# Moving the sample's 32 columns to the second token tile, and a third tile whose two parts share one 512-column product

## The chip, the core and the metric

One core of a Trainium2 chip runs the whole program. The metric is device time in microseconds of one execution, the median over runs. The engines are named as in the profile: PE is the matrix engine (TensorE; its weight loads have a row PEld of their own), DVE is VectorE, ACT is ScalarE, SP issues most of the DMAs.

## The reference

One inference step of a two-layer encoder runs for two groups of tokens that share all weights: 1024 rows of a new stream (the prompt) and 32 rows of a running one (the sample), D = 1024 each. Each layer has a mixer and a feed-forward part, with norms and per-group modulation around them:

```python
for i in range(DEPTH):                      # DEPTH = 2
    mod = jax.nn.silu(c) @ w_ada[i] + b_ada[i]
    h = rmsnorm(x, g_norm[i, 0]) * (1 + sc1) + sh1
    # layer 0: u, v = split(gelu(h @ w_in)); mix = (u * (W_s rmsnorm(v) + b)) @ w_out
    # layer 1: trailing means over 2, 4, 8, 16 rows minus h, a linear map per group
    x = x + gt1 * rmsnorm(mix, g_norm[i, 1])
    h = rmsnorm(x, g_norm[i, 2]) * (1 + sc2) + sh2
    f = jnp.square(jax.nn.relu(h @ ffn_w_up[i])) @ ffn_w_down[i]
    x = x + gt2 * rmsnorm(f, g_norm[i, 3])
```

The sample's pooling also reads 15 cached rows. Outputs are both groups' results, the last 15 pooling inputs of each, and the sample's normalised v rows. All arrays are float32.

## The kernel before

**Layout.** Activations lie transposed: channels on partitions (8 blocks of 128), tokens along the free dimension. Three token tiles are kept in SBUF all the time (`TILES`, line 27): prompt columns 0 to 383, 384 to 767, and 768 to 1023 followed by the 32 sample columns, so 384, 384 and 288 columns. `acc0` to `acc2` hold the residual stream or the running sum of a tile, with 16 columns of halo in front for the pooling.

**Precision.** Every weight block and every activation is split in a rounded large part and a small rest (`hh` and `hl`, `wh` and `wl`). `products` (line 897) makes three matmuls for each term: large by large (line 902), large weight by small activation (903) and small weight by large activation (904), all summed in one PSUM bank. A weight block of 128 x 128 is loaded for each matmul.

**Work.** A feed-forward chunk of 512 hidden channels on one tile is an item, `ffn_item` (line 1281): four up products of 8 terms, each read by ACT (relu, then square) and split into `fh` and `fl`, and eight down products of 4 terms, each added to `acc` by `accumulate` (the first chunk of a layer writes by ACT instead). `sgu_item` (line 1156) does the same for the gating mixer, with the gating products of v between. The down products of an item are emitted behind the first up product of the next item (`pending`, `flush`). `passes` (lines 318 to 325) lists the chunks: in each layer some chunks run on all tiles one after the other, and most run on one tile alone, tile by tile (layer 0: chunks 0, 1 and 4 to 7; layer 1: chunks 0 to 3, and 6 and 7 for the third tile). A weight item is loaded by DMA and split by one ACT and one DVE step of 1024 columns a partition; 16 slots hold 8 such pairs.

**Order.** What lies between the parts of a layer (norms, residual, modulation, pooling, output transposes) is written as generators, the fillers. The emission order is decided while the program is built, by a planner that adds up a matrix-engine time and a DVE time:

```python
def tick(us):
    time["pe"] += us
    time["dve"] = max(time["dve"], time["pe"] - 4.0)
tt = on_dve(nc.vector.tensor_tensor, 0.16, 930.0)   # 0.16 + elements / 930
...
while time["dve"] < time["pe"] and fillers:          # in weave(), after each product
    if not pull():
        break
```

`weave` first takes a weight step from the stream and then pulls filler steps, from the first two fillers in the list, as long as the DVE account is behind. `run_ffn` (line 1539) sees to it that a tile's filler is complete before the tile's first chunk of the next part: if it isn't, the pending down products are flushed and the rest of the filler is emitted there (`finish`). For layer 1, a tile's filler is `to_pool`: residual, norm, pooling, the group products (`pp`, line 1529), then `mix_to_ffn` with a second residual and the modulation that writes `hh` and `hl`. Its steps name the tiles `r_rf`, `r_r_1x`, `r_rp` (norm factors), `xo` (old residual), `win` (windows). The last output blocks are transposed by `turn_last` (`LAST`, line 106) and scaled into `xlast`.

Of the kernel before, what the change touches and what calls it, by code (L numbers as in the profile page):

```python
# [26 lines left out]
TILES = [(0, 384, 0), (384, 384, 0), (768, 256, DEC)]  # L27
# [7 lines left out]
def tile_stream_encoder_step(  # L35
# [66 lines left out]
    acc = [const.tile([P, KB, HALO + n], F32, name=f"acc{t}") for t, n in enumerate(ncol)]  # L102
# [3 lines left out]
    LAST = [(0, 0, P), (P, 0, P), (ncol[-1] - P, P - DEC, DEC)]  # L106
# [5 lines left out]
    one = work.tile([P, 384], F32, tag="c", bufs=3, name="one")  # L112
# [13 lines left out]
    def A(t, kb, c0=0, w=None):  # L126
        w = ncol[t] - c0 if w is None else w
        return acc[t][:, kb, HALO + c0 : HALO + c0 + w]


    def room(part, t, name, dtype=F32):
        return work.tile([P, KB, ncol[t]], dtype, tag=f"h{part}{t}", bufs=1, name=name)

# [9 lines left out]
    def t_m(name):  # L143
        return work.tile([P, 384], F32, tag="m", bufs=3, name=name)

    def t_c(name):
        return work.tile([P, 384], F32, tag="c", bufs=3, name=name)
# [188 lines left out]
    for q in range(4):  # L336
        for j in (8 + 2 * q, 9 + 2 * q, 2 * q, 2 * q + 1):
            add_ada(0, j)
        add_w(*v_item(0, q))
        if q == 0:  # L340
            for b in range(3, 6):
                add_x(b)
    first_ada = len(stream)
    for b in range(6, 9):
        add_x(b)
# [30 lines left out]
    def in_raw(k):  # L376
# [4 lines left out]

    x_rows = [
        room("h", t, f"x_rows{t}")
        .rearrange("p k n -> p (k n)")[:, : ncol[t] // P * D]
        .rearrange("p (b k n) -> p b k n", k=KB, n=P)
        for t in range(NT)
    ]
    junk = room("l", NT - 1, "xsq")
# [176 lines left out]
    def x_squares(b, r):  # L565
# [5 lines left out]
            accum_out=ssx[:nr, b : b + 1],  # L571
        )

    def x_turn(b, r):
        t = min(b // 3, 2)
        c0 = (b - 3 * t) * P
        nr = P if b < 8 else DEC
        for half in range(2):
# [6 lines left out]
            dst = acc[t][:, half * 4 : half * 4 + 4, HALO + c0 : HALO + c0 + nr]  # L585
# [150 lines left out]
    class Stat:  # L736
# [7 lines left out]
        def square(self, k, src=None):  # L744

            if k == 0:
                self.sq = room("l", self.t, f"sq_{self.tag}")
# [27 lines left out]
            if k + w == KB and self.split:  # L775
                self.parts = [
                    work.tile([P, 384], F32R, tag=g, bufs=3, name=f"s{g}_{self.tag}") for g in "cm"
# [12 lines left out]
        def finish(self, out):  # L790
# [7 lines left out]
            r = work.tile([P, 384], F32, tag="rr", bufs=2, name=f"r_{self.tag}")[:, :n]  # L798
# [9 lines left out]
    def residual(st, l, cf, tag, out, store=True, stat=True):  # L808
# [12 lines left out]
        for half in range(2):  # L821
            for k2 in (2 * half, 2 * half + 1):
                load(k2)
            for k2 in (2 * half, 2 * half + 1):
# [12 lines left out]
                a = acc[t][:, 2 * k2 : 2 * k2 + 2, HALO:]  # L837
# [4 lines left out]
        if store:  # L842
            nc.sync.dma_start(xd[t], acc[t][:, :, HALO:])
# [9 lines left out]
    def apply(t, l, cf, sh, r, keep=False):  # L853
        hh[t] = room("h", t, f"hh{l}_{cf}_{t}", F32R)
        hl[t] = room("l", t, f"hl{l}_{cf}_{t}", F32R)
        parts = [[(k, *seg) for seg in segs[t]] for k in range(KB)]
        if keep and len(segs[t]) == 1:
            parts = [parts[k] + parts[k + 1] for k in range(0, KB, 2)]
        for part in parts:
            xs = []  # L860
            for k, c0, w, v in part:
                x = A(t, k, c0, w)
                a = t_m(f"mt{t}_{k}_{v}")[:, :w] if keep else x
# [23 lines left out]
    def first_norm(t):  # L887
        n = ncol[t]
        nb = 3
        cp = t_c(f"r_h0_{t}")  # L890
        got = []
        yield from spread(t, ssx[:, 3 * t : 3 * t + nb], f"h0_{t}", got, cp)
# [4 lines left out]
    def products(ps, n, terms):  # L897

        last = len(terms) - 1
        tick(3 * len(terms) * (0.004 + n / 2265.0))  # L900
        for i, (wh, wl, rh, rl) in enumerate(terms):
            mm(ps[:, :n], wh, rh, start=i == 0, stop=False)  # L902
            mm(ps[:, :n], wh, rl, start=False, stop=False)  # L903
            mm(ps[:, :n], wl, rh, start=False, stop=i == last)  # L904
# [86 lines left out]
    with tc.manual_schedule():  # L991
# [14 lines left out]
        for q in range(4):  # L1006
# [4 lines left out]
            if q == 0:  # L1011
                stream_to("x", 5)
# [3 lines left out]
                next(h1)  # L1016
                x_turns.popleft()()
# [12 lines left out]
        stream_to("x", 8)  # L1030
# [19 lines left out]
    for half in range(2):  # L1050
        x = work.tile([P, 384], F32R, tag="rr", bufs=2, name=f"hs{half}")[:, : 8 * DEC].rearrange(
# [3 lines left out]
        nc.vector.tensor_copy(x[:, :, 0:DEC], hh[NT - 1][:, ks, 256 : 256 + DEC])  # L1055
        nc.vector.tensor_copy(x[:, :, DEC:], hl[NT - 1][:, ks, 256 : 256 + DEC])
# [19 lines left out]
    for p, b in v_order:  # L1076
# [3 lines left out]
        if p == 2 and b < NT:  # L1080
            with tc.issue_after(loads[("v", 2, 3)]):
                nc.sync.dma_start(xd[b], acc[b][:, :, HALO:])
# [34 lines left out]
    def t_hid(kind, name):  # L1117
        return work.tile([P, 384], F32R, tag="h" + kind, bufs=5, name=name)

    def split(dst_hi, dst_lo, src, n):  # L1120
        act(out=dst_hi[:, :n], in_=src[:, :n], func=AF.Copy)  # L1121
        tt(out=dst_lo[:, :n], in0=src[:, :n], in1=dst_hi[:, :n].bitcast(F32), op=ALU.subtract)

    def accumulate(t, d, ps, first):
        n = ncol[t]
        if first:
            act(out=A(t, d), in_=ps[:, :n], func=AF.Copy)
        else:
            tt(out=A(t, d), in0=A(t, d), in1=ps[:, :n], op=ALU.add)

    def up_terms(wkey, t):
        wh, wl = need_w(wkey)
        return [
            (wh[:, k * P : (k + 1) * P], wl[:, k * P : (k + 1) * P], hh[t][:, k, :], hl[t][:, k, :])
# [21 lines left out]
    def sgu_item(p, t, mix, after):  # L1156
# [8 lines left out]
        def inputs(g):  # L1165
# [5 lines left out]
            if nsm:  # L1171
                nc.sync.dma_start(
                    vl[:nsm, nch, :], vd[SEQ : SEQ + nsm, g * 256 : (g + 1) * 256]
                )
# [14 lines left out]
        def up(g, k):  # L1189
# [3 lines left out]
            products(ps, n, up_terms(("u", p, g, k), t))  # L1193
# [5 lines left out]
            act(out=u[:, :n], in_=ps[:, :n], func=AF.Gelu_apprx_tanh)  # L1199
            us.append(u)  # L1200

        def gate(g):
# [4 lines left out]
            for k in range(2):  # L1207
# [10 lines left out]
                if nsm:  # L1218
                    mm(
                        sp[:, npr : npr + nsm],  # L1220
                        vl[:nsm, nch, k * P : (k + 1) * P],
# [4 lines left out]
            for k, sp in enumerate(sps):  # L1226
                f = 2 * g + k
                s = t_c(f"s{g}_{t}_{k}")
                stt(
                    out=s[:, :npr].rearrange("p (c j) -> p c j", j=P),  # L1230
# [438 lines left out]
```

## Time and profile before

| what | value |
|---|---|
| median of 3 runs | 2206.56 us (2206.07 to 2206.97) |
| span of the profiled execution, first to last instruction | 2201.9 us |
| own time of the profiled execution | not recorded beside its span; the median is 4.7 us above the span |
| mean granted PE clock over the span | 0.999 |
| ACT busy | 986.7 us (45%) |
| HBM traffic | 278.95 MB read, 31.84 MB written, 141 GB/s |

A timeline row has the start in us, the length in us, the engine, the line, the operation, what is written from what, shapes, and how many instructions were merged in it. A group row ends in busy us, the mean ns of one, and the idle time before it with what ended it. Line 79 is the helper through which DVE operations are recorded.

### The profile page before, as it was taken

What the parts mean: (1) busy time and instruction counts of PE and PEld (TensorE: products, weight loads), DVE (VectorE), ACT (ScalarE), POOL (GpSimd) and SP (SyncE); (2) the same over time, 40 slices, a digit from 0 to 9 for tenths busy, and PEclk for the clock granted to TensorE, in tenths of its full rate; (3) what the DMA queues carried; (4) which work ended last, traced back from release to release, by engine and by line L of the source; (5) the groups of instructions that cost most, each with busy time, mean ns of one, the idle gap of its engine ahead of it and who ended that gap; (6) DMA issues with size and microseconds to landing.
All of it is one profiled execution on the core that took longest, in us unless ns stands there. A gap on an engine that the chain in (4) does not pass through costs nothing.

```text
span 2201.9 us, 33431 instructions
## 1 busy us (share of the span) xinstructions
PE 2178.7 (99%) x13383; PEld 2096.0 (95%) x13383; DVE 1376.8 (63%) x2433; ACT 986.7 (45%) x1679; POOL 0.7 (0%) x6
## 2 busy tenths in 40 slices
PE   7999999999999999999999999999999999999998
PEld 5777899999999999999999999999999999999998
DVE  5665746566869556575747879879675553523375
ACT  4633422134447552323445566656564542313354
POOL 0000000000000000000000000000000000000000
PEclk9999999999999999999999999999999999999999
DMA  8475624243527443343645465555454552302343
GB/s 296 128 250 165 201 81 135 89 143 113 154 82 222 148 145 124 102 131 122 191 125 153 149 182 177 180 185 159 139 171 143 155 153 66 107 10 77 97 121 111
DMA packets 354976, 312.98 MB, mean 142 GB/s; under 512 B 10818, under 2 KB 316682, under 8 KB 354820
## 3 DMA queue, kind: packets, MB, share of 16 engines
q1 hardware_dynamic: 352676, 309.43, 45.3%
q8 instruction: 105, 1.72, 0.3%
q10 hardware_dynamic: 2144, 1.41, 0.2%
q14 instruction: 51, 0.42, 0.1%
HBM read 278.95 MB, written 31.84 MB: 141 GB/s over the span
## 4 chain that ended last, share of the span: by engine, by line
PE 96%; DMA 2%; DVE 1%; ACT 1%; SPq 0%; issue 0%; ACTq 0%; DVEq 0%
PE pf L902 12%; PE pf L904 11%; PE pg L902 11%; PE pg L904 11%; PE pg L903 11%; PE pf L903 11%; PE pu L902 3%; PE pu L904 3%; PE po L902 3%; PE po L904 3%; PE po L903 3%; PE pu L903 3%; PE pv L929 2%; PE pv L930 2%; PE pv L931 2%; PE psp L1211 1%
## 5 line engine op out<-in xcount | busy, mean ns | idle before, releaser
L902 PE MATMUL pf<-hh,wh_up 128*128 128x384 f32 (+1 forms) x1536 | 502.6, 327 | 0.0
L902 PE MATMUL pg<-fh,wh_dn 128*128 128x384 f32 (+1 forms) x1536 | 498.0, 324 | 0.0
L904 PE MATMUL pf<-hh,wl_up 128*128 128x384 f32 (+1 forms) x1536 | 496.5, 323 | 0.0
L904 PE MATMUL pg<-fh,wl_dn 128*128 128x384 f32 (+1 forms) x1536 | 494.8, 322 | 0.0
L903 PE MATMUL pg<-fl,wh_dn 128*128 128x384 f32 (+1 forms) x1536 | 494.6, 322 | 0.0
L903 PE MATMUL pf<-hl,wh_up 128*128 128x384 f32 (+1 forms) x1536 | 490.5, 319 | 0.0
L902 PEld LDWEIGHTS pg<-fh,wh_dn 128*128 128x128 f32 x1536 | 288.8, 188 | 4.4 <-issue 3.3
L79 DVE TENSOR_TENSOR wl_up<-raw,wh_up 128x1024 fp32r<-128x1024 f32 x152 | 185.9, 1223 | 167.8 <-ACT wh_up L417 167.8
L902 PEld LDWEIGHTS pf<-hh,wh_up 128*128 128x128 f32 x1536 | 288.2, 188 | 1.3 <-issue 0.8
L903 PEld LDWEIGHTS pg<-fl,wh_dn 128*128 128x128 f32 x1536 | 288.6, 188 | 0.7
L903 PEld LDWEIGHTS pf<-hl,wh_up 128*128 128x128 f32 x1536 | 288.6, 188 | 0.4
L904 PEld LDWEIGHTS pg<-fh,wl_dn 128*128 128x128 f32 x1536 | 288.5, 188 | 0.0
L904 PEld LDWEIGHTS pf<-hh,wl_up 128*128 128x128 f32 x1536 | 287.9, 187 | 0.0
L417 ACT ACTIVATE wh_up<-raw 128x1024 fp32r<-128x1024 f32 x152 | 161.1, 1060 | 278.6 <-PE pf L903 214.3
L79 DVE TENSOR_TENSOR acc<-acc,pg 128x384 f32<-128x384 f32 (+1 forms) x336 | 173.9, 518 | 165.7 <-PE pg L904 164.4
L417 ACT ACTIVATE wh_dn<-raw 128x1024 fp32r<-128x1024 f32 x152 | 161.0, 1060 | 217.7 <-PE pg L903 180.4
L79 DVE TENSOR_TENSOR wl_dn<-raw,wh_dn 128x1024 fp32r<-128x1024 f32 x152 | 185.9, 1223 | 85.3 <-ACT wh_dn L417 85.1
L79 DVE SCALAR_TENSOR_TENSOR aa<-raw,csil,aa 128x512 f32<-128x512 f32 (+1 forms) x364 | 204.3, 621 | 1.9 <-DMA raw<-in_w_ada_dram 1.5
L1293 ACT ACTIVATE r<-pf 128x384 f32<-128x384 f32 (+1 forms) x192 | 86.8, 452 | 197.1 <-PE pf L904 191.7
L79 DVE TENSOR_TENSOR fl<-r,fh 128x384 fp32r<-128x384 f32 (+1 forms) x192 | 100.3, 522 | 104.6 <-ACT fh L1121 103.4
L902 PE MATMUL pu<-hh,wh_u 128*128 128x384 f32 (+1 forms) x384 | 128.0, 333 | 0.0
L902 PE MATMUL po<-ush,wh_o 128*128 128x384 f32 (+1 forms) x384 | 124.2, 324 | 0.0
(264 smaller groups left out, 2899.6 us busy)
## 6 DMA issues: line engine op xcount, KB each, us to landing
raw<-in_ffn_w_up_dram SPq DMA_DIRECT2D x152, 512.0 KB, 4.1
raw<-in_ffn_w_down_dram SPq DMA_DIRECT2D x152, 512.0 KB, 3.4
raw<-in_w_ada_dram SPq DMA_DIRECT2D x96, 512.0 KB, 3.9
raw<-in_sgu_w_in_dram SPq DMA_DIRECT2D x40, 512.0 KB, 4.6
xd<-acc SPq DMA_DIRECT2D x8, 1536.0 KB, 7.4
raw<-in_sgu_w_out_dram SPq DMA_DIRECT2D x24, 512.0 KB, 4.1
xo_r<-xd SPq DMA_DIRECT2D x32, 384.0 KB, 3.3
vd<-vt SPq DMA_DIRECT2D x32, 256.0 KB, 3.3
```

The lines of the kernel that those rows point to most:

```text
L79: return op(out, *args, **kw)
L417: act(out=wh, in_=r, func=AF.Copy)
L902: mm(ps[:, :n], wh, rh, start=i == 0, stop=False)
L903: mm(ps[:, :n], wh, rl, start=False, stop=False)
L904: mm(ps[:, :n], wl, rh, start=False, stop=i == last)
L929: mm(ps[:m, :], a_h, wh[:, o : o + 512], start=k == 0, stop=False)
L930: mm(ps[:m, :], a_h, wl[:, o : o + 512], start=False, stop=False)
L931: mm(ps[:m, :], a_l, wh[:, o : o + 512], start=False, stop=k == KB - 1)
L1211: mm(sp[:, c * P : (c + 1) * P], vl[:, c, k * P : (k + 1) * P], wr[:, c * P : (c + 1) * P], start=True, stop=True,)
L1293: act(out=r[:, :n], in_=ps[:, :n], func=AF.Relu)
```

## The change

The 32 sample columns go from the third tile to the second, so the tiles have 384, 416 and 256 columns. For the third tile the large and the small part of an activation are kept side by side (`double_room`, and one `hid` tile per hidden block). The large weight part multiplies both at once, a matmul of 512 columns that fills a PSUM bank; the small weight part multiplies the large activation part, 256 columns, into the first half. The two halves are then added where a sum leaves PSUM: `gather` for up products, two adds in `accumulate` for down products.

```diff
-TILES = [(0, 384, 0), (384, 384, 0), (768, 256, DEC)]
+TILES = [(0, 384, 0), (384, 384, DEC), (768, 256, 0)]
+WIDE = 384 + DEC
+X_ORDER = (0, 1, 2, 3, 4, 5, 8, 6, 7)
...
-    LAST = [(0, 0, P), (P, 0, P), (ncol[-1] - P, P - DEC, DEC)]
+    LAST = [(0, 0, P), (P, 0, P)]
...
-    def products(ps, n, terms):
-
+    def products(t, ps, terms):
+
+        n = ncol[t]
         last = len(terms) - 1
-        tick(3 * len(terms) * (0.004 + n / 2265.0))
+        tick(len(terms) * ((3 if t < NT - 1 else 2) * 0.004 + 3 * n / 2265.0))
         for i, (wh, wl, rh, rl) in enumerate(terms):
-            mm(ps[:, :n], wh, rh, start=i == 0, stop=False)
-            mm(ps[:, :n], wh, rl, start=False, stop=False)
-            mm(ps[:, :n], wl, rh, start=False, stop=i == last)
+            if t < NT - 1:
+                mm(ps[:, :n], wh, rh, start=i == 0, stop=False)
+                mm(ps[:, :n], wh, rl, start=False, stop=False)
+                mm(ps[:, :n], wl, rh, start=False, stop=i == last)
+            elif i < last:
+                mm(ps, wh, rl, start=i == 0, stop=False)
+                mm(ps[:, :n], wl, rh, start=False, stop=False)
+            else:
+                mm(ps[:, :n], wl, rh, start=False, stop=False)
+                mm(ps, wh, rl, start=False, stop=True)
+
+    def gather(t, ps, out, func):
+        n = ncol[t]
+        if t == NT - 1:
+            act(out=out, in_=ps[:, n : 2 * n], func=AF.Copy)
+            tt(out=out, in0=out, in1=ps[:, :n], op=ALU.add)
+            act(out=out, in_=out, func=func)
+        else:
+            act(out=out, in_=ps[:, :n], func=func)
...
     def accumulate(t, d, ps, first):
         n = ncol[t]
+        parts = [ps[:, :n], ps[:, n : 2 * n]] if t == NT - 1 else [ps[:, :n]]
         if first:
-            act(out=A(t, d), in_=ps[:, :n], func=AF.Copy)
-        else:
-            tt(out=A(t, d), in0=A(t, d), in1=ps[:, :n], op=ALU.add)
+            act(out=A(t, d), in_=parts.pop(), func=AF.Copy)
+        for x in parts:
+            tt(out=A(t, d), in0=A(t, d), in1=x, op=ALU.add)
```

In `products`, the operand named `rl` of the third tile is both parts side by side. Along with this:

- The sample's rows are loaded and turned with the second tile's (block 8 ahead of blocks 6 and 7), its first norm and its separate steps (its own coefficients, its cached rows and pooling windows, its state outputs) move to the second tile's norm and filler, and the second tile's output gets a fourth block.
- The 16 halo columns leave `acc`. A `halo` tile carries the end of one tile's pooling input to the next, and the first level of each window is made in two or three steps instead of one.
- The gating step writes its sum back to PSUM and the product to the up tile, where a tile of its own was used before; the sample's rows of v come by a DMA into a tile of their own. Tiles of 384 columns become 416 wide, and one tag has 2 buffers instead of 3.
- The queue of passes, the planner's rules and its DVE constants stay.

More of the change, by code (lines that the diff above doesn't have):

```diff
@@ L860, in apply @@
             xs = []
+            kept = {k: t_m(f"mt{t}_{k}") for k, *_ in part} if keep else {}
             for k, c0, w, v in part:
                 x = A(t, k, c0, w)
-                a = t_m(f"mt{t}_{k}_{v}")[:, :w] if keep else x
+                a = kept[k][:, c0 : c0 + w] if keep else x
                 stt(
@@ L1467, in run @@
-            parts = [(acc[t][:, :, 0 : HALO + npr], npr, 0, "p")]
+            yield 0.5 if nsm or t == NT - 1 else False
+            if nsm or t == NT - 1:
+                if nsm:
+                    src, out_ap, nm = pool_ext["e"][:, :, 32:48], state_pool_sample[0, 0], "s"
+                else:
+                    src, out_ap, nm = acc[t][:, :, npr - 16 : npr], state_pool_prompt[0, 0], "p"
+                for half in range(2):
+                    so = t_x(f"stp_{nm}{half}", [P, 512])
+                    pt = ps_ms(f"stT_{nm}{half}")
+                    tick(0.5)
+                    for i in range(4):
+                        nc.tensor.transpose(
+                            pt[:16, i * P : (i + 1) * P], src[:, half * 4 + i, :], ident
+                        )
+                    nc.vector.tensor_copy(so[:16, :], pt[:16, :])
+                    nc.sync.dma_start(out_ap[:, half * 512 : (half + 1) * 512], so[1:16, :])
+                yield False
```

208 lines of the change are left out of this document (115 added, 93 removed).

## The prediction

> **What bounds the kernel now.** I read the page first, then the timeline of the matrix engine to get the distance between starts of products of each width, then the groups of VectorE and ScalarE with shapes kept apart, then busy time by stretch around the place where layer 0 hands over to layer 1.
>
> ```profile
> span 2201.9 us, 33431 instructions
> ...
> PE 2178.7 (99%) x13383; PEld 2096.0 (95%) x13383; DVE 1376.8 (63%) x2433; ACT 986.7 (45%) x1679; POOL 0.7 (0%) x6
> ...
> PE 96%; DMA 2%; DVE 1%; ACT 1%; SPq 0%; issue 0%; ACTq 0%; DVEq 0%
> ```
>
> The matrix engine is never free and carries 96% of the chain, so the change is worth what it takes from the sequence of products, less whatever makes that sequence wait. The recorded length of a product (0.29 us for 288 columns) overlaps the next one; what counts is the distance between starts:
>
> ```profile
> 799.95 0.29 PE L902 MATMUL pf<-hh,wh_up 128*128 128x288 f32 x1
> ...
> 801.95 0.30 PE L902 MATMUL pf<-hh,wh_up 128*128 128x288 f32 x1
> ...
> 660.20 0.34 PE L902 MATMUL pf<-hh,wh_up 128*128 128x384 f32 x1
> ...
> 663.88 0.34 PE L902 MATMUL pf<-hh,wh_up 128*128 128x384 f32 x1
> ...
> 149.63 0.40 PE L929 MATMUL pv<-wh_v,hh 128*128 128x512 f32 x1
> ...
> 152.41 0.40 PE L929 MATMUL pv<-wh_v,hh 128*128 128x512 f32 x1
> ...
> 2177.11 1.07 PE L1615 MATMUL yT<-ident,acc 128*128 128x128 f32 x8
> 2177.94 0.38 PE L902 MATMUL pg<-fh,wh_dn 128*128 128x288 f32 x1
> ```
>
> 15 products of 288 columns take 2.00 us, 133.3 ns each; 21 of 384 take 3.68 us, 175.2 ns; 12 of 512 take 2.78 us, 231.7 ns; 8 transposes of 128 columns take 0.83 us, 104 ns.
>
> **Products of the third tile.** From 288 to 384 columns a product grows by 41.9 ns in 96 columns, 0.4365 ns a column, and 7.6 ns are left at no columns. The line gives 231.1 ns at 512, and 231.7 was measured, so it holds there; it gives 119.3 ns at 256 and 189.2 ns at 416. One term (a weight block with its two parts) takes 3 x 133.3 + 3 x 175.2 = 925.5 ns on the third and second tile now, and 3 x 189.2 + 231.1 + 119.3 = 918.0 ns after: the columns are the same, one start in six goes, and 7.5 ns with it. The third tile has 2 layers x 8 chunks x 64 terms in the feed-forward part and 256 in the gating mixer (16 products of 8, 32 of 4): 1280 terms, 9.6 us. Bounds: if a 256-column product keeps the 133.3 ns of a 288-column one, 14 ns a term are lost against this, and the sum is 8 us the other way; if it falls to the 104 ns of a transpose, the gain is 29 us. I stay on the line, because the 512 point lies on it.
> The Trainium skill, "TensorE: Matmul & The Clock Gate", section "Wait — 56ns, not 53.3ns?", has starts of warm products apart by columns over 2.4 GHz plus about 2.5 ns. The trace disagrees: 120 + 2.5 against 133.3 ns, 213.3 + 2.5 against 231.7. By that rule a removed start is worth 2.5 ns, 3.2 us in all in place of 9.6.
>
> **What the small engines get.** The third tile's sums now lie in two halves of a PSUM bank. An up product was read by one ScalarE step; now a copy, an add on VectorE, and the function. A down product was added once; now twice.
>
> ```profile
> L79 DVE TENSOR_TENSOR wl_dn<-raw,wh_dn 128x1024 fp32r<-128x1024 f32 x152 | 185.9, 1223 | 85.3 <-ACT wh_dn L417 85.1
> ...
> L79 DVE TENSOR_TENSOR acc<-acc,pg 128x384 f32<-128x384 f32 x224 | 123.7, 552 | 138.0 <-PE pg L904 137.0
> ...
> L79 DVE TENSOR_TENSOR acc<-acc,pg 128x288 f32<-128x288 f32 x112 | 50.3, 450 | 27.7 <-PE pg L904 27.4
> ...
> L79 DVE TENSOR_TENSOR fl<-r,fh 128x288 fp32r<-128x288 f32 x64 | 29.3, 457 | 5.7 <-ACT fh L1121 4.7
> ```
>
> From 384 to 288 columns an add loses 102 ns, so 256 columns take about 416 ns. A third-tile item of the feed-forward part (4 up products, 8 down products, 8 weight splits) holds VectorE for 8 x 1.223 + 8 x 0.450 + 4 x 0.457 = 15.2 us of its 192 x 0.1333 = 25.6 us on the matrix engine. After it is 9.8 + 24 x 0.416 = 19.8 us of 64 x 0.3504 = 22.4 us. Spare VectorE time per item falls from 10.4 to 2.6 us.
>
> Within an item this should still just flow:
>
> ```profile
> 1342.43 0.45 DVE L79 TENSOR_TENSOR acc<-acc,pg 128x288 f32<-128x288 f32 x1
> 1342.80 1.23 DVE L79 TENSOR_TENSOR wl_dn<-raw,wh_dn 128x1024 fp32r<-128x1024 f32 x1
> 1343.93 0.62 DVE L79 SCALAR_TENSOR_TENSOR hl<-acc,mod,hh 128x384 fp32r<-128x384 f32 x1
> ```
>
> Back to back, steps start closer than they last (0.37 for 0.45, 1.13 for 1.23). Two down products take 8 x 0.3504 = 2.80 us; their VectorE work is one split and four adds, 1.13 + 4 x 0.336 = 2.5 us.
>
> ```profile
> L417 ACT ACTIVATE wh_dn<-raw 128x1024 fp32r<-128x1024 f32 x152 | 161.0, 1060 | 217.7 <-PE pg L903 180.4
> ...
> L1121 ACT ACTIVATE fh<-r 128x288 fp32r<-128x288 f32 x64 | 28.5, 445 | 1.8
> L1295 ACT ACTIVATE r<-r 128x288 f32<-128x288 f32 x64 | 28.4, 444 | 1.8
> ...
> L1293 ACT ACTIVATE r<-pf 128x288 f32<-128x288 f32 x64 | 25.3, 395 | 8.1 <-PE pf L904 8.1
> ```
>
> An up product, 2.80 us, has on ScalarE a weight rounding, the copy, the function, the square and the rounding: 1.060 + 0.395 + 2 x 0.444 + 0.445 = 2.79 us by the 288-column rows, a little less at 256. Copy and add, about 1 us, must free the bank before the next product but one, 2.80 us on; a filler or split on VectorE in front of the add eats that cover. I put 1.5 us in all on such waits, between 0 and 20 (1 us in each of the third tile's 20 items).
>
> **Where the lost spare time was used.** The norms, residuals and pooling between the layers ("fillers") run on VectorE beneath products. The sample's share, and the whole sample window, now belong to the second tile's filler, which is due earlier than the third's.
>
> ```profile
> core 0: us, PE busy (x) PEld busy (x) DVE busy (x) ACT busy (x) POOL busy (x), PEclk, DMA share, GB/s
> 1299.30:1407.10 107.80, 107.80 (x777) 107.80 (x776) 91.49 (x138) 68.92 (x112) 0.00 (x0) 1.00 0.67 204
> 1407.10:1545.40 138.30, 138.30 (x794) 133.51 (x794) 116.15 (x194) 90.59 (x160) 0.00 (x0) 1.00 0.54 166
> 1545.40:1564.20 18.80, 18.76 (x114) 17.89 (x114) 12.70 (x19) 5.67 (x7) 0.00 (x0) 1.00 0.39 117
> ```
> ```profile
> 1491.28 0.61 DVE L79 SCALAR_TENSOR_TENSOR sm_rp<-sq_rp,eps,sc_rp 128x384 fp32r<-128x384 f32 x1
> ...
> 1496.58 1.14 DVE L79 SCALAR_TENSOR_TENSOR acc<-acc,coef,r_rp 128x384 f32<-128x384 f32 x2
> ...
> 1539.46 0.61 DVE L79 SCALAR_TENSOR_TENSOR hl<-acc,mod,hh 128x384 fp32r<-128x384 f32 x1
> ...
> 1564.18 0.34 PE L902 MATMUL pf<-hh,wh_up 128*128 128x384 f32 x1
> ```
>
> The three stretches run from the second tile's last layer-0 down products to its first layer-1 product at 1564.18: then come the third tile's four solo chunks, the first tile's four, and the down products that are flushed because the second tile's filler isn't finished. Its last input is written at 1540.1, 24 us ahead. VectorE is busy 220 of 265 us. After, it gets 4 x 4.6 = 18 us more in the third tile's items and some 18 us more in the second tile's filler (40 steps on 32 columns, the sample's windows, wider rows), and the stretch is 4 x 3.2 = 13 us shorter: 256 of 252 us. It no longer fits unless work of the third tile's filler, also in there, gives way.
>
> ```profile
> L79 DVE TENSOR_TENSOR acc<-acc,xo_r 128x768 f32<-128x768 f32 x32 | 30.4, 949 | 0.0
> ...
> L79 DVE SCALAR_TENSOR_TENSOR hl<-acc,mod,hh 128x384 fp32r<-128x384 f32 x32 | 18.8, 615 | 0.2 <-ACT hh L875 0.2
> ...
> L79 DVE SCALAR_TENSOR_TENSOR acc<-acc,coef,r_rp 128x384 f32<-128x384 f32 x16 | 9.3, 612 | 0.0
> L79 DVE TENSOR_TENSOR sq_r_1x<-sq_r_1x 128x768 f32<-128x768 f32 x9 | 8.6, 951 | 0.0
> ...
> L79 DVE SCALAR_TENSOR_TENSOR hl<-acc,mod,hh 128x32 fp32r<-128x32 f32 x16 | 3.9, 246 | 0.0
> ```
>
> How late it gets is set by the order in which the program's planner emits steps, so I redo its accounts with its own constants, which decide order and stand for no time of mine. An item's 64 terms count 3 x (0.004 + columns/2265) each, its VectorE steps 0.16 + elements/930: 33.3 - 17.0 = 16.3 us are spare at 384 columns, 25.2 - 15.7 = 9.5 at 288, 36.0 - 17.4 = 18.6 at 416 and 22.2 - 20.5 = 1.7 at 256; the last chunk gives some 3.5 to its squares, and a layer's first chunk gains 4.6, since ScalarE writes its sums. Between the first tile's layer 0 and the second tile's layer 1 that is 4 x 16.3 + 34 + 70 = 169 us now (second tile's items, third's, first's) for the steps of the first and the second tile's filler, 66 + 65 = 131. After it is 74 + 3 + 70 = 147 for 67 + 80 = 147. The 38 us of slack that waits and the third tile's filler used are gone, so the second tile's filler should be about 38 planner-us behind when its first item comes. The flushed down products supply 7; what is left, 31, is the filler's entire last part, the residual and the modulation (15.2 + 2.6 + 13.0), and the program then forces it out with nothing else for the matrix engine. On VectorE it is 8 x (0.612 + 0.246) + 4 x 1.02 + (3 x 1.02 + 1.2) + 16 x (0.615 + 0.246) = 29 us of recorded lengths (1.02 is 0.95 widened to 832 columns; 1.2 is for two steps of one width, by the 0.55 and 0.61 us rows), about 24 us at back-to-back spacing (57 steps, 0.085 us each). The first up product, 24 x 0.189 = 4.5 us, follows block by block beneath its end, and the 6 us that VectorE idles in the flushed stretch take some; from the last square to the first scaled step 5.3 us passed in the trace (1491.28 to 1496.58), part of it other work, and I add 4 for that chain. Stall: 24 - 4.5 - 6 + 4 = 17.5, say 18 us, between 0 and 36 (no packing ahead, pooling late too).
>
> **The rest.**
>
> ```profile
> 2195.16 4.19 DVE L79 SCALAR_TENSOR_TENSOR xlast<-yT,r_last,xlast 128x512 f32<-128x512 f32 x6
> ...
> L79 DVE SCALAR_TENSOR_TENSOR hl<-mt,mod,hh 128x32 fp32r<-128x32 f32 x8 | 2.0, 244 | 0.0
> ```
>
> Behind the last product six scaled adds become four, 4.19 x 2/6 = 1.4 us less; a second accumulate adds 0.3: 1.1 us gained. The third tile's final transposes fall from 24 to 16 twice and the second's output rises by 8: 8 x 104 ns = 0.9 us gained. At the start the sample joins the second tile's first norm: 16 VectorE steps of 0.244 us, 3.9 us, partly beneath weights that are being loaded; I take 1 of 0 to 3.9, as products there wait for inputs only at block edges. Moved DMAs (the sample's rows ahead of blocks 6 and 7, the sample's gating rows in a load of their own) are as many as before and small; nothing for them.
>
> Sum: -9.6 - 0.9 - 1.1 + 1 + 1.5 + 18 = +8.9 us on a span of 2201.9. The median of the runs is 2206.56, 4.7 us above the span; the profile carries no time of its own execution, so I add the change to the median: 2215.5 us.
>
> **Rivals.** *It fits* (faster): VectorE's real steps are shorter than the planner's constants (1.13 for 1.26 us), so the forced part may run early in real gaps, and the third tile's filler gives way. Its place is the second tile's first layer-1 product; it decides if the delay stays below the 24 us of cover. Then the stall is 0 and the time 2206.6 - 11.6 + 2.5 = 2197.5. For it: 45 idle us in the three stretches; against: much of that idleness is waiting in the filler's own chain, which doesn't pack. *Half a stall*: 6 to 14 us, 2204 to 2211, no change to be measured. *The weight load bounds the narrow product*: a 256-column product can't go below the load of the next weights; at 133.3 ns a term loses 14 ns, 18 us, and even without the stall the time is 2215. Against it: transposes, with as large a load each, start 104 ns apart, below 119. The Trainium skill, same page, section "LDWEIGHTS (loading the stationary operand)", has 128 columns load in 128/1.2 = 106.7 ns; by it 119 ns clears the load, and the trace's 104 ns agree. *Banks come free late* in every third-tile item: 20 x 1 us, about 2216 without the big stall, more with it.
>
> **How the numbers follow.** The stall decides: 0.50 for a stall of 14 us or more, 2211 to 2236; 0.25 for it fits; 0.15 for half a stall; 0.05 each for the load and for the banks. The range from 2196 to 2236 runs over all of them; the likeliest case alone spans 2211 to 2236. A measurement here can tell about 0.2%, 4.4 us, from no change. Faster by more than that is it fits, 0.25; within, half a stall, 0.15; slower, the other three, 0.60.
>
> **What would show it.** Starts 512 columns apart by 229 to 232 ns and 256 by 118 to 121 in the third tile's items; a third-tile chunk of 22.4 us; VectorE at nine tenths there; and one gap of 10 to 30 us on the matrix engine ahead of the second tile's first layer-1 up product, ended by VectorE or ScalarE writing its input. Wrong if that gap isn't there, or if the gaps lie between third-tile products and end at the accumulate or the gather.

## The result, and the profile after

The changed kernel takes 2243.05 us (median of 4 runs, 2241.23 to 2244.38) against 2206.4 us of the kernel before on the same chip: a ratio of 1.0165, 95% interval 1.0151 to 1.0179. It is slower, as forecast, but by 36.7 us where 8.9 were forecast, and outside the range of 2196 to 2236 us. The page of the profile after:

```profile
span 2239.4 us, 31192 instructions
...
PE 2184.1 (98%) x12091; PEld 2029.6 (91%) x12091; DVE 1458.6 (65%) x2713; ACT 1011.0 (45%) x1753; POOL 0.7 (0%) x6
...
PEclk9999999999999999999999999999799999999999
...
PE 92%; DVE 3%; DMA 2%; ACT 1%; issue 1%; ACTq 0%; DVEq 0%; SPq 0%
```

There are 1292 products fewer, yet the matrix engine is busy 5 us longer; VectorE has 82 us more work; and one slice in 40 has a granted clock of 7 tenths. Line 81 is here the helper for VectorE steps that was line 79. The matrix engine's waits (engine, tile and line waiting, releaser, us in total, times, longest) begin with a new one:

```profile
PE pn_r_1x L809 <- ACT sc_r_1x L794: 23.3, 1, 23.3
...
PE pf L923 <- ACT hh L894: 3.9, 1, 3.9
...
PE pg L930 <- ACT f L1160: 0.7, 1, 0.7
PE pg L927 <- DVE acc L81: 0.7, 1, 0.7
```

Both large ones lie at one place, ahead of the second tile's first layer-1 up product. The timeline of the matrix engine there:

```profile
1570.89 0.34 PE L925 MATMUL pg<-f,wl_dn 128*128 128x384 f32 x1
1571.06 0.35 PE L809 MATMUL pn_rp<-sc_rp,ones 128*128 128x416 f32 x1
1571.26 0.45 PE L809 MATMUL pn_rp<-sm_rp,ones 128*128 128x416 f32 x1
1594.99 0.72 PE L809 MATMUL pn_r_1x<-sc_r_1x,ones 128*128 128x416 f32 x1 [23.29 <-ACT sc_r_1x L794]
1595.68 0.72 PE L809 MATMUL pn_r_1x<-sm_r_1x,ones 128*128 128x416 f32 x1
1600.35 1.06 PE L923 MATMUL pf<-hh,wh_up 128*128 128x416 f32 x2 [3.95 <-ACT hh L894]
...
1604.21 0.35 PE L924 MATMUL pf<-hl,wh_up 128*128 128x416 f32 x1
```

From 1571.3 to 1600.35 the engine has two small products to do (the two `pn_r_1x`). The norm of the mixer's output (`rp`) has only just been summed, so residual, second norm and modulation all lie in the gap. VectorE does this in it:

```profile
1571.11 0.69 DVE L81 SCALAR_TENSOR_TENSOR acc<-win2p,acc 128x512 f32<-128x512 f32 x1
...
1572.18 0.68 DVE L81 TENSOR_TENSOR win2p<-acc 128x510 f32<-128x510 f32 x1
...
1578.34 0.61 DVE L81 SCALAR_TENSOR_TENSOR acc<-acc,coef,r_rp 128x384 f32<-128x384 f32 x1
...
1583.03 1.02 DVE L81 TENSOR_TENSOR acc<-acc,xo_r 128x832 f32<-128x832 f32 x1 [0.18 <-DMA xo_r<-xd]
...
1592.62 1.65 DVE L81 TENSOR_TENSOR sq_r_1x<-sq_r_1x 128x832 f32<-128x832 f32 x2 [0.96 <-ACT sq_r_1x L763]
1594.98 0.65 DVE L81 SCALAR_TENSOR_TENSOR sm_r_1x<-sq_r_1x,eps,sc_r_1x 128x416 fp32r<-128x416 f32 x1 [0.71 <-ACT sc_r_1x L794]
1597.56 0.59 DVE L81 SCALAR_TENSOR_TENSOR q_r_1x<-pn_r_1x,q_r_1x 128x416 f32<-128x416 f32 x1 [1.94 <-ACT q_r_1x L814]
```

The steps named `win2p` are the third tile's windows: they stand in the queue between the second tile's steps. From 1571.4 to 1600.3 some 17 us are the second tile's own steps, 6 us the third tile's windows, 1.6 us a weight split and an add, and 4 us idle time in the chain, of which the three bracketed waits for ScalarE make 3.6.

### The profile page after: what moved, and what is told of

Same layout as the page of the kernel before. It is cut to its first block, busy times and chain, and to the rows that moved or that the text cites. A ratio compares the mean times of both kernels' runs of the same rounds, so it can differ in the third digit from the quotient of the medians.

```text
span 2239.4 us, 31192 instructions
## 1 busy us (share of the span) xinstructions
PE 2184.1 (98%) x12091; PEld 2029.6 (91%) x12091; DVE 1458.6 (65%) x2713; ACT 1011.0 (45%) x1753; POOL 0.7 (0%) x6
## 4 chain that ended last, share of the span: by engine, by line
PE 92%; DVE 3%; DMA 2%; ACT 1%; issue 1%; ACTq 0%; DVEq 0%; SPq 0%
PE pf L923 8%; PE pg L923 8%; PE pg L924 8%; PE pg L925 8%; PE pf L925 8%; PE pf L924 8%; PE pf L927 4%; PE pg L927 4%; PE pf L928 2%; PE pu L923 2%; PE pv L965 2%; PE pu L925 2%; PE po L923 2%; PE po L925 2%; PE po L924 2%; PE pu L924 2%
## 5 line engine op out<-in xcount | busy, mean ns | idle before, releaser
L923 PE MATMUL pf<-hh,wh_up 128*128 128x416 f32 (+1 forms) x1024 | 356.5, 349 | 4.6 <-ACT hh L894 3.9
L923 PE MATMUL pg<-f,wh_dn 128*128 128x416 f32 (+1 forms) x1024 | 356.5, 348 | 0.4 <-ACT f L1160 0.4
L925 PE MATMUL pf<-hh,wl_up 128*128 128x416 f32 (+1 forms) x1024 | 353.2, 345 | 0.0
L925 PE MATMUL pg<-f,wl_dn 128*128 128x416 f32 (+1 forms) x1024 | 351.3, 343 | 0.0
L924 PE MATMUL pf<-hl,wh_up 128*128 128x416 f32 (+1 forms) x1024 | 350.5, 343 | 0.0
L924 PE MATMUL pg<-f,wh_dn 128*128 128x416 f32 (+1 forms) x1024 | 350.2, 342 | 0.2 <-DVE f L81 0.2
L81 DVE TENSOR_TENSOR acc<-acc,pg 128x256 f32<-128x256 f32 (+2 forms) x464 | 219.2, 488 | 145.5 <-PE pg L925 123.0
L923 PEld LDWEIGHTS pg<-f,wh_dn 128*128 128x128 f32 x1024 | 192.5, 188 | 6.3 <-issue 3.6
L924 PEld LDWEIGHTS pg<-f,wh_dn 128*128 128x128 f32 x1024 | 192.2, 188 | 3.2 <-issue 0.5
L925 PEld LDWEIGHTS pg<-f,wl_dn 128*128 128x128 f32 x1024 | 191.9, 187 | 0.2
L927 PE MATMUL pf<-hd,wh_up 128*128 128x512 f32 x448 | 160.7, 397 | 0.0
L927 PE MATMUL pg<-f,wh_dn 128*128 128x512 f32 x384 | 142.4, 397 | 0.7 <-DVE acc L81 0.7
```

Of the source, the lines that this page charges most:

```text
L81: return op(out, *args, **kw)
L927: mm(ps, wh, rl, start=i == 0, stop=False)
```

## Experiments

The theory to test (A): the added VectorE steps, and what the planner books for them, push the second tile's filler back until it is forced out with nothing to cover it. Rivals: the sample's move does it alone (B); PSUM banks held longer and ScalarE's copies do it (C). "Forced" steps are those that `finish` pulls ahead of the second tile's first layer-1 chunk, counted while the program is built: 36 in the changed kernel, 0 in the kernel before. The chips' own runs of the kernel before had medians of 2206.5 to 2206.8 us.

### Three products in place of the double one

```diff
-            elif i < last:
-                mm(ps, wh, rl, start=i == 0, stop=False)
...
+            if t == NT - 1:
+                rl = rl[:, n : 2 * n]
+            mm(ps[:, :n], wh, rh, start=i == 0, stop=False)
+            mm(ps[:, :n], wh, rl, start=False, stop=False)
+            mm(ps[:, :n], wl, rh, start=False, stop=i == last)
```

`gather` and `accumulate` read one half again. 4 steps are forced.

> The changed kernel with the third tile's terms as three products of 256 columns again (no double product, no copy in gather, no second add in accumulate); the sample stays in the second tile. Theory A (the 28 us gap ahead of the second tile's first layer-1 up product comes from the doubled VectorE adds, which eat the spare time in which the emission order places the second tile's filler): the gap falls under 8 us; products are worth about 0 against before (three starts of 116 to 119 ns and no 512), the start keeps its +4 us: 2206 to 2216 us. Theory B (the sample's move alone makes the filler late, the adds don't matter): the gap stays at 20 us or more, 2230 to 2245 us.

Measured: 2202.71 us (10 runs), ratio 0.9982 (0.9972 to 0.9991). The list of waits has no row for `pn_r_1x` or `pf` any more: there is no gap. The sample's move alone (with its windows and halo steps) costs nothing; it is worth 4 us, and the time lies 3.3 us below what A gave. B falls.

### The double product, one half read

```diff
-            act(out=out, in_=ps[:, n : 2 * n], func=AF.Copy)
-            tt(out=out, in0=out, in1=ps[:, :n], op=ALU.add)
-            act(out=out, in_=out, func=func)
+        act(out=out, in_=ps[:, :n], func=func)
...
-        parts = [ps[:, :n], ps[:, n : 2 * n]] if t == NT - 1 else [ps[:, :n]]
+        parts = [ps[:, :n]]
```

> The changed kernel with every product as it is, but only the first half of each third-tile bank is read (no copy in gather, no second add): large activation by large weight plus the small weight's part, so the part from the small activations of the third tile is left out of the result. Theory A: the gap goes as in the run with three products, and the 0.8 us waits for banks in the third tile's items go too; the double products' worth stays: 2202 to 2210 us. Theory B: 2230 us or more. Theory C (the gap is not the adds but the slower turn of banks and ScalarE's longer chain): as A here, so this run alone doesn't part A from C; the next one does.

Measured: 2204.21 us (10 runs), ratio 0.9985 (0.9976 to 0.9995). Without the adds the gap is gone (4 forced steps), as A and C say. But 1280 starts fewer than in the run with three products brought nothing: 1.5 us more, where 7.5 ns for each would be 9.6 us less. The starts of one third-tile item and of the next show it, in the kernel before, after, with three products, and with one half read (the rows are the first up product of layer 1's third and fourth chunk on this tile):

```profile
1748.39 0.30 PE L902 MATMUL pf<-hh,wh_up 128*128 128x288 f32 x1
...
1773.82 0.30 PE L902 MATMUL pf<-hh,wh_up 128*128 128x288 f32 x1
```
```profile
1792.31 0.47 PE L927 MATMUL pf<-hd,wh_up 128*128 128x512 f32 x1
...
1815.12 0.47 PE L927 MATMUL pf<-hd,wh_up 128*128 128x512 f32 x1
```
```profile
1757.38 0.28 PE L924 MATMUL pf<-hd,wh_up 128*128 128x256 f32 x1
...
1779.78 0.28 PE L924 MATMUL pf<-hd,wh_up 128*128 128x256 f32 x1
```
```profile
1755.39 0.40 PE L927 MATMUL pf<-hd,wh_up 128*128 128x512 f32 x1
...
1777.89 0.40 PE L927 MATMUL pf<-hd,wh_up 128*128 128x512 f32 x1
```

25.43 us become 22.81; but three plain products of 256 columns take 22.40, and the double form without its adds 22.50. The narrower tile shortens the item; the double form doesn't.

### One number of the planner

```diff
-    tt = on_dve(nc.vector.tensor_tensor, 0.16, 930.0)
-    stt = on_dve(nc.vector.scalar_tensor_tensor, 0.16, 840.0)
+    tt = on_dve(nc.vector.tensor_tensor, 0.05, 930.0)
+    stt = on_dve(nc.vector.scalar_tensor_tensor, 0.05, 840.0)
```

> The changed kernel with one number altered, the fixed cost that the emission planner books for each VectorE step, 0.16 to 0.05 us (back-to-back steps in the trace are 0.34 us apart at 256, 0.46 at 384 and 1.13 at 1024 columns, against 0.44, 0.57 and 1.26 booked). Every instruction stays, only their order moves. Theory A1 (a matter of order: VectorE has the time, the filler is only emitted too late): the gap of 28 us vanishes, what is left of the change is +5 to +10 us: 2209 to 2217 us. Theory A2 (VectorE really lacks the time between the layers): the gap turns into waits of the same sum at third-tile accumulates or at the same place, 2230 us or more.

Measured: 2219.55 us, ratio 1.0055 (1.0040 to 1.0070). With the same instructions in another order the gap is gone (no step is forced), and 23.5 us with it. VectorE, with all of the second tile's filler now ahead of its first layer-1 product (the last input is written by 1540.0), is busy 229 of the 250 us from the second tile's last layer-0 down products to that product, so it had the time:

```profile
1316.60:1566.90 250.30, 245.82 (x1349) 223.24 (x1348) 229.03 (x443) 161.61 (x293) 0.00 (x0) 1.00 0.55 167
```

(The columns are those of the prediction's table of stretches; VectorE is the third busy time.) The run is 2.5 us above the top of what A1 gave; the controls below bear on that.

### The third tile's filler held back

```diff
-            f = next((f for f in list(fillers)[:2] if open_(f)), None)
+            f = next((f for f in list(fillers)[: 1 if fillers and fillers[0][0] == "ffn1_1" else 2] if open_(f)), None)
```

> The changed kernel, but while the second tile's filler is the first in the list, the third tile's filler is not pulled. Theory A3 (a good part of the gap, 10 to 13 us, is the third tile's window steps queued on VectorE in front of the forced part): the gap ahead of the second tile's first layer-1 up product shrinks to 12 to 20 us, and the third tile's filler in turn is late by up to 10 us: 2230 to 2243 us in all. If the third tile's steps had only used time that was idle anyway: the gap stays at 26 us or more, 2243 us or above.

Measured: 2245.36 us, ratio 1.0174 (1.0157 to 1.0191). The gap shrinks and a new one opens ahead of the third tile:

```profile
PE pn_r_1x L809 <- ACT sc_r_1x L794: 14.4, 1, 14.4
...
PE pf L923 <- ACT hh L894: 3.9, 1, 3.9
PE pf L927 <- DVE hd L81: 3.6, 1, 3.6
...
PE pn_r_2x L809 <- ACT sc_r_2x L794: 2.1, 1, 2.1
```

27.2 us of waits become 18.3, as A3 said, and the third tile's filler now makes 5.7 us of its own. So the third tile's steps were part of the gap, some 9 us, but holding them back only moves the debt. The total still lies above A3's range, at 2243 us or more as in the other case, though the gap did not stay. No run shows what made up the difference; the clock was at half a second time, from 1753.4 to 1763.6.

### Only the up products, or only the down products, double

```diff
+    def products(t, ps, terms, two=False):
...
-            products(t, ps, up_terms(("up", p, j), t))
+            products(t, ps, up_terms(("up", p, j), t), t == NT - 1)
...
+                products(t, ps, terms, False)
```

and the reverse for the second run. 10 and 12 steps are forced.

> The changed kernel, but only the third tile's up products are double (with copy and add in gather); its down products are three of 256 columns with one add. In the runs before, a term of three 256-column products took 361.0 ns among up products and 344.4 ns among down products, a double term 352.5 and 353.2. Theory P (the double form is worth 8.5 ns a term in the up products and costs 8.8 ns in the down products, 640 terms of each): -5.4 us on the 2202.7 us of three products, and 10 filler steps are now forced ahead of the second tile's first layer-1 product, a gap of 3 to 12 us: 2203 to 2212 us. Rival (each term worth 7.5 ns of either kind): -4.8 us here too, so only the next run parts them.

> The counterpart: only the third tile's down products are double (two adds in accumulate), its up products are three of 256 columns, read by one step. Theory P: +5.6 us on the 2202.7 us of three products, and 12 filler steps forced, a gap of 3 to 12 us: 2212 to 2222 us; down terms of 353 ns. Rival (7.5 ns a term): -4.8 us and the same gap, 2202 to 2211 us; down terms under 345 ns.

Measured: up products double 2212.76 us, ratio 1.0028 (1.0017 to 1.0038); down products double 2220.07 us, ratio 1.0060 (1.0043 to 1.0077). At that place both have one wait of the same length:

```profile
PE pf L925 <- ACT hh L894: 5.1, 1, 5.1
```

The up run lies just above its range, the down run in P's and far from the rival's. Mean distance from one start to the next over all feed-forward products of a kind, in ns, worked out from the traces with distances over 0.4 us left out, and the sum for a third-tile term:

| kernel | up, 256 | up, 512 | up term | down, 256 | down, 512 | down term |
|---|---|---|---|---|---|---|
| before (288) | 133.3 | | 399.9 | 132.3 | | 396.9 |
| three products | 120.2 | | 360.6 | 114.8 | | 344.4 |
| one half read | 117.7 | 235.0 | 352.7 | 119.4 | 234.0 | 353.4 |
| after | 116.8 | 234.6 | 351.4 | 123.2 | 235.3 | 358.5 |
| up double | 116.9 | 235.2 | 352.1 | 117.1 | | 351.3 |
| down double | 120.2 | | 360.6 | 119.5 | 234.0 | 353.5 |

Against three products a double term saves 8 to 9 ns among up products, and costs 9 ns among down products with one half read and with only these double, 14 in the changed kernel. The means hold short waits too: the middle distance (median) behind a 256-column down product is 118 ns in the changed kernel as with one half read, and 113 and 114 ns where the means are 114.8 and 117.1. By the medians the form saves 10 ns an up term (117 + 233 for 3 x 120) and costs 12 a down term (118 + 233 for 3 x 113), as P says in kind. Why the next product starts sooner behind a 256-column one among down products than among up products, no run shows.

### The adds alone

```diff
             act(out=r[:, :n], in_=ps[:, :n], func=AF.Relu)
+            if t == NT - 1:
+                tt(out=r[:, :n], in0=r[:, :n], in1=r[:, :n], op=ALU.max)
...
             tt(out=A(t, d), in0=A(t, d), in1=ps[:, :n], op=ALU.add)
+        if t == NT - 1:
+            tt(out=A(t, d), in0=A(t, d), in1=A(t, d), op=ALU.max)
```

This was run on the kernel before and on the one with three products. In the mixer only the accumulates get a step.

> The kernel before (sample in the third tile, three products of 288) with harmless VectorE steps added: a maximum of a tile with itself behind each up product's first read and behind each accumulate of the third tile, as many steps as the change adds there (4 and 8 an item), reading no PSUM bank. Theory A (the adds load VectorE and push the second tile's filler back; each alone a part, with the sample's steps the whole): 12 filler steps are forced, a gap of 4 to 12 us ahead of the second tile's first layer-1 product, 2211 to 2222 us. Rival (without the sample's steps no filler is late; banks held longer are what costs): 2205 to 2209 us.

> The kernel with three products of 256 columns in the third tile (2202.7 us) with the harmless VectorE steps of the run before added there (a maximum of a tile with itself, 4 and 8 an item): no double product, no copy in gather, no second read of a bank, only VectorE time as in the changed kernel. 34 filler steps are forced in the planner's order, 36 in the changed kernel. Theory A (VectorE steps and the order they cause are the whole loss): a gap of 20 to 30 us ahead of the second tile's first layer-1 product, 2236 to 2246 us. Rival (the double form's banks and ScalarE's copies make a good part): under 2228 us.

Measured on the kernel before: 2216.41 us, ratio 1.0046 (1.0031 to 1.0061), in A's range, though the waits at that place are short ones of 1.0 us and less. Behind them the clock was at half from 1571.6 to 1578.4, where 19 products of 384 columns took 6.5 us and 175 ns each would make 3.3. Up to 2.7 us of that are the clock's, since the tile's last input was written by 1579.75 and the product that waits for it started at 1582.45; the rest is spread. Measured with the sample in the second tile: 2238.61 us, ratio 1.0147 (1.0132 to 1.0162), with the same two waits as in the changed kernel:

```profile
PE pn_r_1x L809 <- ACT sc_r_1x L794: 20.3, 1, 20.3
...
PE pf L924 <- ACT hh L894: 4.0, 1, 4.0
```

So plain VectorE steps, with the planner's time booked for them, with no double product and no bank held, bring 35.9 us on 2202.7, of the 40.3 us by which the changed kernel is above it; C is left with 4 us at most. The adds cost 9.9 us where the sample lies in the third tile and 35.9 where it lies in the second: neither edit alone makes the large gap.

### Can the order be mended?

Three controls, with the 0.05 us only on three products, on the version with double up products, and only between the layers (`fillers[0]` is the first or second tile's), and one with 0.08 us for the second tile's filler on three products. The first two change the two numbers as above; the last two are made like this:

```diff
-            time["dve"] += fixed + n / rate
+            time["dve"] += (0.05 if ahead() else fixed) + n / rate
```

> Only the up products double, and the planner's fixed cost per VectorE step 0.05 in place of 0.16, so that no filler step is forced. Theory P with A1: the gap is gone, a third of the 15 us of small waits that the full double form had at this planner rate stays: 2198 to 2206 us, perhaps the fastest version. If the small waits come with the moved order and not with the adds: 2208 us or more.

> A control for the planner's number: three products, and 0.05 us in place of 0.16 per VectorE step, so the order moves where no stall is to be removed. If the moved order costs by itself (the filler's own chain then runs too early and the matrix engine waits inside it): 2207 to 2215 us, and so the 15 us that the full double form still lost at this number are largely the number's. If it costs nothing: 2201 to 2205 us, and those 15 us belong to the added VectorE steps.

> The changed kernel with the planner's 0.05 us only while the first or second tile's filler between the layers is first in the list, and 0.16 elsewhere. No step is forced. Theory A1: the gap goes, and the waits that the number brought in the layer-0 and final parts don't come: 2210 to 2218 us. If VectorE lacks the time in just this stretch: 2219 us or more, as waits within it.

> Three products of 256 columns, and the planner's 0.08 us while the second tile's filler is first in the list, so that its last 4 steps are no longer forced and no down products are flushed. If the flush still cost something: 2198 to 2201 us, the fastest version. If it was hidden: 2201.5 to 2205 us, as three products without it.

Measured: double up products at 0.05 us 2215.54, ratio 1.0040 (1.0025 to 1.0055), 2.8 us slower than at 0.16, so the small waits come with the moved order; three products at 0.05 us 2225.45, ratio 1.0086 (1.0071 to 1.0101), 22.7 us slower than at 0.16 and above both ranges; the changed kernel with the number between the layers only 2217.75, ratio 1.0049 (1.0033 to 1.0066), at the top of A1's range; three products without the forced steps 2208.23, ratio 1.0007 (0.9997 to 1.0016), again above both ranges. No order tried was better than the one with 0.16 where nothing large is forced. In three products at 0.05 us the matrix engine waits in many small places:

```profile
PE pf L924 <- ACT wh_up L427: 2.6, 2, 1.8
PE pf L924 <- ACT r L930: 2.5, 1, 2.5
PE pf L926 <- DVE wl_up L81: 1.9, 2, 1.7
...
PE pn_r_1x L809 <- ACT sc_r_1x L794: 1.7, 2, 1.2
```

The longest wait for a small weight part, 1.7 us, ends at a split that stood behind window steps of a filler on VectorE; the two for a large part end at a rounding that itself waited 0.8 and 1.8 us for the weight's DMA; and a filler's own products (`pn_r_1x`) stop the matrix engine when they are emitted ahead of their input. How the 22.7 us divide among such causes is not shown. The 15 us between the changed kernel at 0.05 us and one half read are less than what the number costs three products by itself, so they need no lack of VectorE time; that they are the number's alone is not shown. Whether an order exists that removes the gap at no price was not found. Four steps forced behind flushed down products (three products) cost less than the order without them, and three products show no wait at that place: that small flush was hidden.

The fastest version run is three products with the sample in the second tile, 2202.71 us, ahead of both kernels, by 0.18% of the kernel before.

## Why the prediction was wrong in size

**The sum by its terms.** *Products, -9.6 us forecast, about +0.7 measured.* The distances forecast for the feed-forward part were each within 5 ns in the mean (231.1 for 512 columns against 234.6 and 235.3; 119.3 for 256 against 116.8 and 123.2; 189.2 for 416 against 190.4 and 189.2), though for 512 and 256 columns outside the bands named as signs. But the term's worth of 7.5 ns was a difference of five such numbers. With the measured means an up term on both tiles goes from 926.7 ns (399.9 + 3 x 175.6) to 922.6, a down term from 920.1 (396.9 + 3 x 174.4) to 926.1: 512 terms each, and 128 each in the mixer from 939.6 to 936.3 and from 918.9 to 919.8, make +0.7 us, of which 1.0 is the slow products behind the gap. "I stay on the line, because the 512 point lies on it" is the first step that failed, in size: that point came from the gating products of another part of the program, with other neighbours, and the rows for 288 and 384 columns were all of up products, while a down term took 920.1 ns before, not 925.5. Its own bound, 14 ns a term the other way, was nearer, by its number only: no 256-column product kept 133 ns. The rule of the Trainium skill weighed there ("TensorE: Matmul & The Clock Gate", section "Wait — 56ns, not 53.3ns?"), 2.5 ns for a start removed, came nearer with its -3.2 us; its distances are too short all the same, by it 215.8 ns at 512 columns where the trace has 234.6.

*The stall, 18 us forecast, 28.5 measured*, 23.3 and 3.9 of it in the two waits, the rest in the small products between. Place, releaser and cause were right. The second step that failed, in size, is its credits. The 6 us of idle VectorE time in the flushed stretch gave nothing: from 1545.0 to 1571.3 the third tile's filler ran for some 8 us, VectorE still stood idle for 6.6, and the norm's sum on which the forced part hangs was ready only at its end (`rp` above). And some 6 us of the third tile's windows, for which the forecast had no term, stood in the queue of the gap itself, with 1.6 us of other work. The forced part was 39 us in the planner's account, not 31. In the run that held the third tile's filler back the two waits were 18.3 us. One slip is small: 8 x 104 ns of transposes are 0.8 us, not 0.9.

**The reason that didn't hold.** VectorE was forecast to be overfull, 256 of 252 us, in the three stretches ahead of that place. Busy time by stretch after (VectorE is the third busy time):

```profile
1311.60:1412.00 100.40, 99.70 (x560) 88.72 (x559) 85.40 (x148) 65.70 (x117) 0.00 (x0) 1.00 0.62 182
1412.00:1545.00 133.00, 132.96 (x765) 130.24 (x764) 110.41 (x207) 78.62 (x133) 0.00 (x0) 1.00 0.54 163
1545.00:1571.30 26.30, 26.30 (x125) 20.80 (x123) 19.67 (x38) 16.53 (x31) 0.00 (x0) 1.00 0.39 118
```

VectorE worked 215.5 of 259.7 us: 44 us stood idle while the filler was late, more than the 25 us that it then worked in the gap. The delay was one of order, as the redone account said, and not of capacity; the run with one planner number shows it, since the gap went with no instruction changed and VectorE did all of that work in 229 of 250 us.

**Smaller terms.** The extra add was put at 416 ns; it took 415. Late banks, 1.5 us: the two waits of 0.7 us above. Third-tile items were to show VectorE at nine tenths: it was busy 17.66 of 22.81 us in one item alone, and 20.54 us of a stretch of 21.40 where fillers ran too. The item took 22.8 us for 22.4. At the start +1 was forecast; the first feed-forward item began 5.7 us later than before, but it also began 3.0 us later in the kernel before with adds, which differs there only in the mixer, 3.6 in the run with one half read and 6.4 with three products, so 2 to 3 us can't be told apart there. The end was 4.2 us shorter from the last item's first product on, of which a shorter item makes 2.6.

**What makes up the difference.** Of the 27.8 us between 8.9 and 36.7, the products make 9, the gap 10.5 and the slow products behind it, told below, 2; the remaining 6 are in the start and in small waits, too small to be put to one cause.

**The rivals.** *It fits* and *half a stall* fell with the gap. *The weight load bounds the narrow product* fell: 114.8 ns were reached. *Banks come free late* was small. No rival had the products worth nothing with a full stall, and that, with the longer gap, is what left the range.

## What to carry to other kernels

Before a rewrite that saves starts, take the distance between starts from products of the same kind in the same place; a saving that is a difference of several nearly equal numbers is not known until it is run, and here cutting one edit out (three products) showed at once that the form was worth nothing. Where an emission order is made by accounts, ask of each edit how many booked microseconds of a filler it pushes behind its due place: it is hidden for a few steps and then costs all at once (4 forced steps nothing, 10 and 12 up to 5 us, 34 and 36 more than 24 us). Two edits that draw on the same slack, here the adds at a cost of 9.9 us and the sample's move at a gain of 4, can cost 32 together (2238.6 against 2206.6 us).

## What the runs showed of the hardware

Behind the gap the products are slow. The granted clock (last but two of the columns) around it:

```profile
1575.00:1580.00 5.00, 0.00 (x0) 0.00 (x0) 5.00 (x12) 0.00 (x0) 0.00 (x0) 0.68 0.36 105
1580.00:1590.00 10.00, 0.00 (x0) 0.00 (x0) 9.82 (x21) 2.69 (x3) 0.00 (x0) 0.50 0.70 213
...
1602.00:1604.00 2.00, 2.00 (x7) 1.42 (x6) 2.00 (x7) 1.55 (x4) 0.00 (x0) 0.50 0.00 0
1604.00:1606.00 2.00, 2.00 (x12) 1.98 (x11) 2.00 (x7) 1.00 (x3) 0.00 (x0) 0.98 0.00 0
```

If the clock is either full or half, 0.68 over 5 us puts the fall at about 1576.8, some 5 us after the end of the last product, at 1571.7; it is full again at 1604.1, 3.7 us after products came again at 1600.35. In between ten products of 416 columns took 3.86 us where 190 ns each make 1.9: about 2 us more, of which three short waits make 0.5. This was not in the forecast. The Trainium skill, "TensorE: Matmul & The Clock Gate", section "Part 1: The HAM clock gate (the "warmup" mystery)", has the clock drop to half after an idle window of about 3.4 us and come back after as long a busy one; the trace agrees in that neither came sooner.

Little of these 2 us is the clock's in the end, for VectorE was still writing the inputs of these products:

```profile
1608.50 1.47 DVE L81 SCALAR_TENSOR_TENSOR hl<-acc,mod,hh 128x384 fp32r<-128x384 f32 x4
```
```profile
1610.08 0.55 PE L924 MATMUL pf<-hl,wh_up 128*128 128x416 f32 x2
```

The last small part was written by 1609.97, and the product that waits for it, the second of the two, started at 1610.27. At full clock the engine could have been at most some 0.3 us further there.

A short gap can lose more by the clock than a long one. Where only the up products are double, the engine waited 5.1 us, products came again at 1571.26, and the clock was at half until 1577.8, 6.5 us on:

```profile
1571.30:1577.80 6.50, 6.50 (x18) 5.57 (x19) 6.50 (x19) 3.72 (x10) 0.00 (x0) 0.50 0.01 3
```

The 18 products recorded there would have taken 3.4 us at 190 ns each. The last small part was written by 1580.9, and the product that waits for it started at 1582.5, so up to 1.6 us are the clock's there; that may be part of why this run lies above its range.
